# Sums of gated tiles: accumulating transfers into DRAM in place of VectorE additions

## The chip, the core and the metric

The kernel runs on one core of a Trainium2 chip. A core has TensorE (PE: matrix products into the accumulator memory PSUM), VectorE (DVE), ScalarE (ACT) and GpSimd (POOL) for work element by element, and SyncE (SP), which here only issues transfers. All of them run side by side, each works through its own queue in order, and they wait for one another by semaphores. A transfer (DMA) is carried out by 16 DMA engines once its issuing engine has reached it in its queue; a semaphore tells when it has landed. Working memory is SBUF with 128 partitions; DRAM is the large memory of the chip.

The metric is the time of one execution on the chip in microseconds (us). The three runs of the kernel before gave 1491.32, 1491.71 and 1492.59 us, median 1491.71.

## What is computed

A bidirectional encoder layer runs on two requests with shared weights: `x_prompt` (512 tokens) and `x_sample` (1024 tokens), both 1024 wide. The part that matters here is the feed-forward block at the end:

```python
x = x + jnp.concatenate([a_out, c], axis=-1) @ w_out[l]
h = _rmsnorm(x, norm_ffn_g[l])
u = _dwconv(h @ w_up[l], ffn_dw_w[l], ffn_dw_b[l])        # 3 taps along the tokens
x = x + (jax.nn.silu(u[..., :D_FF]) * u[..., D_FF:]) @ w_down[l]
return _rmsnorm(x, norm_final_g)
```

`D_FF` is 2816, that is 22 blocks of 128 columns, each with a gate half and a value half in `w_up`. Everything is float32; the products are made from two rounded parts of each operand, as three matrix products.

## The kernel before

**Stages.** The input projection, the attention and the convolution come first, then the prompt's up-projection, then the output projection of the sample, the sample's up-projection (a loop over the 22 blocks j, about 765 to 1135 us), and last the down-projection of both requests. This case is about the last two.

**Strassen's method.** Both of these stages multiply 2x2 blocks of matrices with seven products instead of eight (the form of Winograd). For the up-projection of a block j the seven products `first` to `seventh` are each twelve matmuls (four chunks of 128, three products of parts). Their order on PE is written out by hand, in the loop `for j in range(2, NJ)`: second(j), sixth(j), first(j+1), seventh(j), fifth(j+1), fourth(j), third(j). Their weight operands are sums of blocks of `w_up`: `sums_up` makes the sums on VectorE, and `split_up(j, i)` makes the two parts for product i: ScalarE casts the block (L1215), GpSimd subtracts the cast from the block (`sub` with `nc.gpsimd`, L1092). The raw weights are fetched three blocks ahead by `load_up` (L1179).

**Gate and value.** When the products of block j are there, `gate_part(j)` applies the convolution's taps to the gate half (`dwconv`, L1357 to L1359) and makes the tanh (L1366). One iteration later `value_part(j)` does the same for the value half and multiplies: L1376, `dwconv`, L1378. The result `t` is a tile of 128 columns (as partitions) by 1024 tokens; `L` and `R` are its two halves of 512 tokens.

**The sums in question.** For the down-projection, two neighbouring blocks (a pair p, even block e and odd block t) are the four quarters of a 2x2 block matrix: e[L], e[R], t[L], t[R]. Its seven products need seven operands per pair: three of the quarters themselves (e[L] as 1, t[L] as 2, t[R] as 4) and four sums of them (numbers 5, 7, 6, 3). In the kernel before, the even block's tile is kept in `even[p]`, and after the odd block VectorE makes the four sums; SP stores all seven in DRAM, each as a tensor of its own, `ga[i, p]`, 256 KB:

```python
add(x[:, R], e[:, R], t[:, R])          # 5
sub(x[:, L], e[:, L], e[:, R])          # 7
sub(e[:, R], x[:, R], e[:, L])          # 6
sub(y[:], t[:, L], e[:, R])             # 3
for i, b in ((5, x[:, R]), (7, x[:, L]), (6, e[:, R]), (3, y[:])):
    nc.sync.dma_start(ga[i, p][:], b)
```

`add` is L1089 and `sub` is L1092, helpers that many places call, so these lines stand for more than these sums. For the prompt's tokens `pair_sums` makes the same kind of sums on GpSimd (L1023 to L1029) into `gb`.

**Buffers.** `Slots` hands out SBUF buffers of fixed sizes by a list of the free ones: of those large enough it takes the smallest size, and in it the one that came back first (`next(...)` over `free`, and `give` appends). Tiles of 4 KB per partition take a `q` (4096 bytes) when one is free, else a `c` (4224 bytes). A buffer comes back when Python drops the last name of its tile; the new owner's first writer then waits for the old owner's last access. In an iteration the order of the 4 KB tiles is: two for `split_up(j+1, 1, 2)`, one for product 5, then in `value_part(j-1)` the value half's convolution tile, then one each for `split_up(j+1, 6)` and `split_up(j+1, 7)`, the two of `gate_part(j)`, and one each for products 4 and 3.

**Order of the work.** In this stage only PE's order is written by hand (`manual_schedule`); in the last block SP's as well. The orders of ACT, DVE, POOL and SP come from a planner that simulates the program, with dependences by tile, before it is compiled, and are fixed from then on.

**The down-projection.** `ahead` lists the loads of operands in the order of the products 1, 2, 5, 6, 7, 4, 3, for each of the eleven pairs; `load_next` issues them on SP (L1517 for operands of `ga`), long before `operands` uses them. `group` and `mm_down` run the products (L1579 to L1581), and `evacuate(i, w, z)` adds the product of PSUM to the running sums in SBUF.

Of the kernel before, what the change touches and what calls it, by code (L numbers as in the profile page):

```python
# [9 lines left out]
F32 = mybir.dt.float32  # L10
# [3 lines left out]
ALU = mybir.AluOpType  # L14

P = 128
D = 1024
KC = D // P
NT = 512
# [154 lines left out]
def tile_hybrid_encoder(ctx: ExitStack, tc: tile.TileContext, xs, xsT, rel_bias, norm_attn_g, w_in,  # L174
                        attn_sink, w_out, norm_ffn_g, w_up, w_down, norm_final_g, packed, onehot, outs):
    nc = tc.nc
# [5 lines left out]
    dr = ctx.enter_context(tc.tile_pool(name="dr", bufs=1, space=bass.MemoryType.DRAM))  # L182
# [8 lines left out]
    sb = Slots(lambda tag: homes[tag[0]], dict(q=(15, 4096), c=(4, 4224), h=(61, 2048), d=(2, 2176), s=(32, 64)), "q", KEEP)  # L191
# [793 lines left out]
    NPAIR = NJ // 2  # L985
# [4 lines left out]
    HL, HR = slice(0, HT), slice(HT, NT)  # L990

    def gate(j, a, b):
        th, t = bank("gate"), sb.tile([NT])
        nc.scalar.activation(th[:], a[:], AF.Tanh, scale=0.5)
        if j % 4 == VG:
            nc.vector.scalar_tensor_tensor(th[:], th[:], 1.0, a[:], op0=ALU.add, op1=ALU.mult)
            nc.vector.tensor_tensor(t[:], th[:], b[:], op=ALU.mult)
        else:
            nc.vector.scalar_tensor_tensor(t[:], th[:], 1.0, a[:], op0=ALU.add, op1=ALU.mult)
            nc.gpsimd.tensor_tensor(t[:], t[:], b[:], op=ALU.mult)  # L1000
        nc.sync.dma_start(gt[j // 2][:, j % 2, :], t[:])
        if j // 2 < SOON or j // 2 == NPAIR - 1:
            return
        if j % 2 == 0:
            evens[j // 2] = t
        else:
            for _ in pair_sums(j // 2, evens.pop(j // 2), t):
                pass
# [4 lines left out]
    def pair_sums(p, e=None, o=None):  # L1013
        if e is None:
            g = sb.tile([2, NT], among="c")
            nc.sync.dma_start(g[:], gt[p][:])
            yield 0.0
            yield 0.0
            e, o = g[:, 0, :], g[:, 1, :]
        r = sb.tile([4, HT], among="c")  # L1020
        gp = nc.gpsimd.tensor_tensor
        with tc.issue_after(ended["pool"]):
            gp(r[:, 0, :], e[:, HR], o[:, HR], op=ALU.add)  # L1023
        yield 0.0
        gp(r[:, 1, :], e[:, HL], e[:, HR], op=ALU.subtract)
        yield 0.0
        gp(r[:, 2, :], r[:, 0, :], e[:, HL], op=ALU.subtract)
        yield 0.0
        gp(r[:, 3, :], o[:, HL], r[:, 2, :], op=ALU.subtract)  # L1029
        nc.sync.dma_start(gb[p][:], r[:])  # L1030
        yield 0.0

# [52 lines left out]
    W2 = 2 * NT  # L1085
    L, R = slice(0, NT), slice(NT, W2)

    def add(out, a, b, eng=None):
        (eng or nc.vector).tensor_tensor(out, a, b, op=ALU.add)  # L1089

    def sub(out, a, b, eng=None):
        (eng or nc.vector).tensor_tensor(out, a, b, op=ALU.subtract)  # L1092
# [154 lines left out]

    side.extend((right_halves(), conv_norm(4 + NE)))
    side.extend(pair_sums(p) for p in (*range(SOON), NPAIR - 1))
    pace.update(rate=2.2)  # L1250
    for i in range(4, NB - 2):
# [41 lines left out]
    def wide():  # L1293
        return wide_banks.tile([W2])

    ga = {(i, p): dr.tile([P, NT], F32, name=f"ga{i}_{p}") for i in range(1, 8) for p in range(NPAIR)}
    st = {}

    def pair_banks(j):
# [54 lines left out]
    def dwconv(src, f):  # L1354
        w = lambda t: fw[:, t * 44 + f:t * 44 + f + 1]
        u = sb.tile([W2])
        nc.scalar.activation(u[:], src[:], AF.Identity, scale=w(1), bias=fb[:, f:f + 1])  # L1357
        nc.vector.scalar_tensor_tensor(u[:, 1:W2], src[:, 0:W2 - 1], w(0), u[:, 1:W2], op0=ALU.mult, op1=ALU.add)
        nc.vector.scalar_tensor_tensor(u[:, 0:W2 - 1], src[:, 1:W2], w(2), u[:, 0:W2 - 1], op0=ALU.mult, op1=ALU.add)  # L1359
        return u  # L1360
# [4 lines left out]
        t = s["t"] = sb.tile([W2])  # L1365
        nc.scalar.activation(t[:], ug[:], AF.Tanh, scale=0.5)  # L1366

    even = {}

    def value_part(j):  # L1370
        if j < 0:
            return
        p = j // 2
        s = st.pop(j)
        ug, t = s["ug"], s["t"]
        nc.vector.scalar_tensor_tensor(t[:], t[:], 1.0, ug[:], op0=ALU.add, op1=ALU.mult)  # L1376
        uv = dwconv(s.pop("wy"), NJ + j)
        nc.vector.tensor_tensor(t[:], t[:], uv[:], op=ALU.mult)  # L1378
        del ug, uv
        s.clear()  # L1380
        if j % 2 == 0:
            even[p] = t
            nc.sync.dma_start(ga[1, p][:], t[:, L])
            return
        e, x, y = even.pop(p), sb.tile([W2]), sb.tile([NT])
        for i, blk in ((2, L), (4, R)):
            nc.sync.dma_start(ga[i, p][:], t[:, blk])
        add(x[:, R], e[:, R], t[:, R])
        sub(x[:, L], e[:, L], e[:, R])
        sub(e[:, R], x[:, R], e[:, L])  # L1390
        sub(y[:], t[:, L], e[:, R])
        for i, b in ((5, x[:, R]), (7, x[:, L]), (6, e[:, R]), (3, y[:])):
            nc.sync.dma_start(ga[i, p][:], b)

# [79 lines left out]
    first(2)  # L1476
    split_up(2, 6)
    value_part(0)
    third(1)
    split_up(2, 7)  # L1480
# [10 lines left out]
    def load_next(n):  # L1491
        for _ in range(n):
            if ahead:
                key, p = ahead.popleft()
                roomy = sum(f[0][0] in "qc" for f in sb.free) > 5
                if (key, p) in second_half:
                    t = second_half.pop((key, p))
                elif key in BRIEF and p % 2 == 0 and p + 1 < NPAIR and roomy:
                    both = sb.tile([2, NT])
                    t, second_half[key, p + 1] = Part(both, 0), Part(both, 1)  # L1500
                    both = None
                else:
                    t = sb.tile([NT])
                pr[key, p] = t
                what, i, n2 = key
                if what == "a":
                    src = ga[i, p][:]
                elif what == "g":
                    n = min(2, NPAIR - 2 * p)
                    for q in range(n):  # L1510
                        j, h = {1: (0, HL), 2: (1, HL), 4: (1, HR)}.get(i, (0, None))
                        src = gb[2 * p + q][:, GB[i], :] if h is None else gt[2 * p + q][:, j, h]
                        nc.sync.dma_start(t[:, q * HT:(q + 1) * HT], src)
                    continue
                else:
                    src = w_down[0, (2 * p + i) * P:(2 * p + i + 1) * P, n2 * NT:(n2 + 1) * NT]
                nc.sync.dma_start(t[:], src)  # L1517
# [16 lines left out]
    def operands(i, p):  # L1534

        while (("a", i, 0), p) not in pr or (i in need and (need[i], p) not in pr) or \
                (p % 2 == 0 and (("g", i, 0), p // 2) not in pr):
            load_next(1)
# [54 lines left out]
    acc = {}  # L1593

    def evacuate(i, w, z):
        def at(name):
            return acc.setdefault(name, {})

        def fresh(name):
            t = at(name)[w] = sb.tile([W2])  # L1600
            return t

        if i == 1:
            nc.scalar.copy(fresh("u")[:], z[:])
        elif i == 2:
            add(fresh("o11")[:], z[:], acc["u"][w][:])
        elif i == 5:
            nc.scalar.copy(fresh("e")[:], z[:])
        else:
            u = acc["u"][w]  # L1610
            add(u[:], z[:], u[:])
            if i == 6:
                add(fresh("o12")[:], u[:], acc["e"][w][:], nc.gpsimd)
            elif i == 7:
                add(acc["e"][w][:], u[:], acc["e"][w][:], nc.gpsimd)

    def with_x(name, t, n):
        x = xd.pop((t, n))
# [45 lines left out]
    def group(i, p, w, lead=LEAD):  # L1664

        k = ORDER.index(i) * NPAIR + p
        if len(pr) < CAP and sum(f[0][0] == "h" for f in sb.free) > ROOM:
            load_next(1)
        make(k + lead)
        if w not in pd:  # L1670
            pd[w] = wide()
        for q in range(2):
            mm_down(pd[w][:, q * NT:(q + 1) * NT], i, p, 2 * w + q)
        left[i, p] = left.get((i, p), NW3) - 1
        if left[i, p] == 0:
            hl.pop((i, p))
            if p % 2 == 1 or p == NPAIR - 1:
                hp.pop((i, p // 2))
        if p == NPAIR - 1:
            evacuate(i, w, pd.pop(w))  # L1680
# [34 lines left out]
    for j in range(2, NJ):  # L1715
# [5 lines left out]
        if j >= NJ - 2:  # L1721
            load_next(4)
# [3 lines left out]
        sixth(j)  # L1726
        split_up(j + 1, 5)
        value_part(j - 1)
        last = j == NJ - 1
        if last:  # L1730
# [19 lines left out]
    fill((3, 0), (3, 1), (4, 0), (4, 1))  # L1750
    sb.free.extend(raws.free)
    value_part(NJ - 1)

    for i in ORDER[:-1]:
        product(i)
    with_x("u", 1, 0)
    u, e, o11, o12 = (acc.pop(n) for n in ("u", "e", "o11", "o12"))
# [26 lines left out]
    for tt in (2, 3):  # L1784
        z = wide()
# [60 lines left out]
```

## Time and profile before

| What | us |
|---|---|
| median of three runs | 1491.71 |
| the profiled execution, by its own time | 1492.24 |
| its span, first to last instruction | 1490.4 |
| TensorE busy | 1471.8 |
| VectorE busy | 1136.2 |
| ScalarE busy | 798.0 |
| GpSimd busy | 678.0 |

The granted clock of TensorE was 0.998 of full speed in the mean. DRAM was read with 165.29 MB and written with 60.05 MB. Every transfer of the program is issued by SP; GpSimd issues none.

How to read the rows: a busy time is that of the engine's own instructions; issuing a transfer and waiting don't count as busy. In rows by group the mean duration of one instruction is in ns. `q<-h,q 128x512` says which kind of buffer is written and which are read, and how large. `[0.72 <-DMA ga<-q]` at the end of a row is the time that the engine had stood idle before it and what ended that: here the landing of a transfer from a q tile to `ga`. A matmul's row lasts 0.39 us because matmuls are pipelined; the next one starts much sooner.

### The profile page before, as it was taken

Reading aid. Unit: us, or ns where it says so; the run is one execution under the profiler, and the core shown is the slowest. Engines: PE = TensorE matmul, PEld = TensorE weight load, DVE = VectorE, ACT = ScalarE, POOL = GpSimd, SP = SyncE. Lnnn points to the kernel's source line nnn. Section 1 sums busy time; section 2 is a strip of 40 time slices with the busy share of each in tenths; the row PEclk is TensorE's granted clock in tenths of the full one; section 3 lists DMA queues with packets and bytes.
Section 4 is the critical chain, followed back from the end, with each engine's and each line's share of the span. In section 5 each row is a group of like instructions: output and inputs, shape, how many; then the busy total and the mean of one; then the engine's idle time right before and its main releaser. Section 6 shows DMA issues by size and latency. Waiting matters only on the chain.

```text
span 1490.4 us, 19857 instructions
## 1 busy us (share of the span) xinstructions
PE 1471.8 (99%) x6808; PEld 1218.8 (82%) x6808; DVE 1136.2 (76%) x1616; ACT 798.0 (54%) x1417; POOL 678.0 (45%) x540
## 2 busy tenths in 40 slices
PE   9999999999999999999999999999999999999998
PEld 7788887887888888878888888888887888888886
DVE  5999996888689975666868777777776945569884
ACT  8555656345777776444465544555445633444254
POOL 6962335235665575763326555555544000003345
PEclk9999999999999999999999999999999999999999
DMA  9953246374433347883213333333332672357644
GB/s 316 284 171 92 86 121 184 99 231 128 133 110 121 120 126 224 272 304 131 82 57 106 106 106 106 106 104 99 103 105 80 227 265 85 113 171 233 216 163 170
DMA packets 221905, 225.60 MB, mean 151 GB/s; under 512 B 12347, under 2 KB 161859, under 8 KB 221676
## 3 DMA queue, kind: packets, MB, share of 16 engines
q1 hardware_dynamic: 221804, 224.34, 47.0%
q8 instruction: 53, 0.87, 0.3%
q14 instruction: 48, 0.39, 0.1%
HBM read 165.29 MB, written 60.05 MB: 151 GB/s over the span
## 4 chain that ended last, share of the span: by engine, by line
PE 86%; DMA 5%; DVE 3%; POOL 2%; ACT 1%; issue 1%; SPq 0%; POOLq 0%; ACTq 0%; DVEq 0%
PE w L1229 9%; PE w L1231 9%; PE w L1230 9%; PE w L1580 7%; PE w L1579 7%; PE w L1581 7%; PE u L347 4%; PE u L348 4%; PE u L350 4%; PE b L347 4%; PE b L350 4%; PE b L348 4%; DMA c<-gt 2%; PE u L840 2%; PE u L842 2%; PE u L841 2%
## 5 line engine op out<-in xcount | busy, mean ns | idle before, releaser
L231 POOL TENSOR_TENSOR q<-q,q 128x1024 fp32r<-128x1024 f32 x71 | 172.9, 2439 | 122.8 <-ACT q L230 51.4
L1092 POOL TENSOR_TENSOR q<-q,q 128x512 fp32r<-128x512 f32 x101 | 141.5, 1408 | 151.2 <-ACT q L1215 140.3
L1092 DVE TENSOR_TENSOR h<-h,h 128x512 fp32r<-128x512 f32 (+2 forms) x202 | 157.4, 814 | 65.6 <-ACT h L1096 27.8
L1581 PE MATMUL w<-h,h 128*128 128x512 f32 x462 | 179.7, 389 | 0.0
L1579 PE MATMUL w<-h,h 128*128 128x512 f32 x458 | 178.2, 389 | 0.0
L1580 PE MATMUL w<-h,h 128*128 128x512 f32 x458 | 178.2, 389 | 0.0
L1229 PE MATMUL w<-h,q 128*128 128x512 f32 x448 | 174.9, 390 | 1.3 <-ACT w L1312 1.1
L1231 PE MATMUL w<-h,q 128*128 128x512 f32 x448 | 174.3, 389 | 0.0
L1230 PE MATMUL w<-h,q 128*128 128x512 f32 x426 | 165.8, 389 | 0.0
L402 DVE SCALAR_TENSOR_TENSOR c<-c,cvw,c 128x512 f32<-128x512 f32 x209 | 157.0, 751 | 3.1
L347 PE MATMUL u<-h,q 128*128 128x512 f32 x368 | 146.9, 399 | 1.9 <-DVE h L969 1.9
L348 PE MATMUL u<-h,q 128*128 128x512 f32 x368 | 144.0, 391 | 0.0
L350 PE MATMUL u<-h,q 128*128 128x512 f32 x360 | 141.2, 392 | 0.0
L1089 POOL TENSOR_TENSOR q<-q,q 128x1024 f32<-128x1024 f32 x12 | 33.1, 2772 | 229.4 <-DVE q L1089 212.9
L1096 ACT CAST h<-h 128x512 fp32r<-128x512 f32 x120 | 72.1, 622 | 97.1 <-DVE h L1092 40.5
L347 PE MATMUL b<-h,q 128*128 128x512 f32 x264 | 104.9, 397 | 0.9 <-DVE q L437 0.9
L230 ACT CAST q<-q 128x1024 fp32r<-128x1024 f32 (+1 forms) x73 | 75.7, 1041 | 54.5 <-POOL q L231 20.6
L348 PE MATMUL b<-h,q 128*128 128x512 f32 x264 | 103.7, 393 | 0.0
L350 PE MATMUL b<-h,q 128*128 128x512 f32 x264 | 103.5, 393 | 0.0
L1581 PEld LDWEIGHTS w<-h,h 128*128 128x128 f32 x462 | 86.7, 188 | 18.0
L1579 PEld LDWEIGHTS w<-h,h 128*128 128x128 f32 x458 | 86.0, 188 | 18.0
L1580 PEld LDWEIGHTS w<-h,h 128*128 128x128 f32 x458 | 86.0, 188 | 17.7
(443 smaller groups left out, 3625.1 us busy)
## 6 DMA issues: line engine op xcount, KB each, us to landing
q<-in_w_up SPq DMA_DIRECT2D x88, 512.0 KB, 4.3
ga<-q SPq DMA_DIRECT2D x64, 256.0 KB, 2.0
h<-ga SPq DMA_DIRECT2D x57, 256.0 KB, 3.4
q<-in_w_in SPq DMA_DIRECT2D x28, 512.0 KB, 5.1
h<-in_w_down SPq DMA_DIRECT2D x52, 256.0 KB, 4.0
q<-in_x_sample SPq DMA_DIRECT2D x15, 512.0 KB, 6.2
h<-qsd SPq DMA_DIRECT2D x23, 256.0 KB, 3.3
x1d<-q SPq DMA_DIRECT2D x11, 512.0 KB, 5.2
```

The costliest lines, as they stand in the source:

```text
L231: ins = (nc.vector if dve else nc.gpsimd).tensor_tensor(lo[:], raw[:], hi[:].bitcast(F32), op=ALU.subtract)
L347: nc.tensor.matmul(out, whi[:, kc, :], hi[:], start=(kc == 0), stop=False)
L348: nc.tensor.matmul(out, whi[:, kc, :], lo[:], start=False, stop=False)
L350: nc.tensor.matmul(out, wlo[:, kc, :], hi[:], start=False, stop=(kc == KC - 1))
L402: nc.vector.scalar_tensor_tensor(acc[:], src(t), w(t), acc[:], op0=ALU.mult, op1=ALU.add)
L1092: (eng or nc.vector).tensor_tensor(out, a, b, op=ALU.subtract)
L1229: nc.tensor.matmul(out, whi[:, s], hi[:], start=(start and c == 0), stop=False, **go)
L1230: nc.tensor.matmul(out, whi[:, s], lo[:], start=False, stop=False, **go)
L1231: nc.tensor.matmul(out, wlo[:, s], hi[:], start=False, stop=(stop and c == 3), **go)
L1579: nc.tensor.matmul(out, sh[:, c], th[:], start=(p == 0), stop=False)
L1580: nc.tensor.matmul(out, sh[:, c], tl[:], start=False, stop=False)
L1581: nc.tensor.matmul(out, sl[:, c], th[:], start=False, stop=(p == NPAIR - 1))
```

## The change

For the sample's pairs the four sums are no longer made by VectorE. DRAM has a tensor `gs[p]` with four planes of 512 tokens for each pair. After the even block SP stores e[L] into the planes 0, 1 and 2 at once (one transfer that reads its source three times, 768 KB) and e[R] into plane 3. Then GpSimd issues a transfer that adds e[R] to the planes 0, 1 and 2 (`accum_op=ALU.add`). After the odd block GpSimd issues two more: t[R] is added to the planes 1, 2 and 3, and t[L] to plane 2. So the planes become e[L]+e[R], e[L]+e[R]+t[R], e[L]+e[R]+t[R]+t[L] and e[R]+t[R]. The operands 1, 2 and 4 are stored as before.

Compared with the sums before, e[L] and e[R] enter with the same sign in place of opposite ones: the second token half is turned, and so are the products that have it. `evacuate` takes that back by subtracting where it added, and `pair_sums` makes the prompt's sums with the same signs. The tile `even[p]` is no longer kept, and the tiles `x` and `y` are not needed.

```diff
@@ pair_sums
-        gp(r[:, 1, :], e[:, HL], e[:, HR], op=ALU.subtract)
+        gp(r[:, 1, :], e[:, HL], e[:, HR], op=ALU.add)
...
-        gp(r[:, 2, :], r[:, 0, :], e[:, HL], op=ALU.subtract)
+        gp(r[:, 2, :], r[:, 0, :], e[:, HL], op=ALU.add)
...
-        gp(r[:, 3, :], o[:, HL], r[:, 2, :], op=ALU.subtract)
+        gp(r[:, 3, :], o[:, HL], r[:, 2, :], op=ALU.add)
@@
-    ga = {(i, p): dr.tile([P, NT], F32, name=f"ga{i}_{p}") for i in range(1, 8) for p in range(NPAIR)}
+    ga = {(i, p): dr.tile([P, NT], F32, name=f"ga{i}_{p}") for i in (1, 2, 4) for p in range(NPAIR)}
+    gs = [dr.tile([P, 4, NT], F32, name=f"gs{p}") for p in range(NPAIR)]
+    GS = {7: 0, 6: 1, 3: 2, 5: 3}
@@
-    even = {}
+    def into(out, src):
+        nc.gpsimd.dma_start(out, src, accum_op=ALU.add)
+
+    def three(src):
+        return src.unsqueeze(1).to_broadcast([P, 3, NT])
@@ value_part
         if j % 2 == 0:
-            even[p] = t
             nc.sync.dma_start(ga[1, p][:], t[:, L])
+            nc.sync.dma_start(gs[p][:, 0:3, :], three(t[:, L]))
+            nc.sync.dma_start(gs[p][:, 3, :], t[:, R])
+            into(gs[p][:, 0:3, :], three(t[:, R]))
             return
-        e, x, y = even.pop(p), sb.tile([W2]), sb.tile([NT])
         for i, blk in ((2, L), (4, R)):
             nc.sync.dma_start(ga[i, p][:], t[:, blk])
-        add(x[:, R], e[:, R], t[:, R])
-        sub(x[:, L], e[:, L], e[:, R])
-        sub(e[:, R], x[:, R], e[:, L])
-        sub(y[:], t[:, L], e[:, R])
-        for i, b in ((5, x[:, R]), (7, x[:, L]), (6, e[:, R]), (3, y[:])):
-            nc.sync.dma_start(ga[i, p][:], b)
+        into(gs[p][:, 1:4, :], three(t[:, R]))
+        into(gs[p][:, 2, :], t[:, L])
@@ load_next
-                    src = ga[i, p][:]
+                    src = gs[p][:, GS[i], :] if i in GS else ga[i, p][:]
@@ evacuate
             u = acc["u"][w]
-            add(u[:], z[:], u[:])
             if i == 6:
-                add(fresh("o12")[:], u[:], acc["e"][w][:], nc.gpsimd)
+                sub(u[:], u[:], z[:])
+                sub(fresh("o12")[:], u[:], acc["e"][w][:], nc.gpsimd)
             elif i == 7:
-                add(acc["e"][w][:], u[:], acc["e"][w][:], nc.gpsimd)
+                add(u[:], z[:], u[:])
+                sub(acc["e"][w][:], acc["e"][w][:], u[:], nc.gpsimd)
+            else:
+                sub(u[:], z[:], u[:])
```

## The prediction

> **What bounds the kernel now.** I read the page first, then busy time by stretch, then what PE waited for, then the middle stage in order of time. The page:
>
> ```profile
> span 1490.4 us, 19857 instructions
> PE 1471.8 (99%) x6808; PEld 1218.8 (82%) x6808; DVE 1136.2 (76%) x1616; ACT 798.0 (54%) x1417; POOL 678.0 (45%) x540
> ```
>
> TensorE is busy for all but 18.6 us. The change touches the loop over the sample's 22 column blocks, and by signs and sources the stage behind it. The windows view (stretch, length, then busy us of each engine):
>
> ```profile
> 806.00:1120.00 314.00, 314.00 (x1386) 259.96 (x1386) 241.11 (x229) 158.83 (x231) 167.06 (x118) 1.00 0.32 103
> 1110.00:1135.00 25.00, 23.94 (x106) 19.49 (x105) 12.05 (x12) 12.43 (x19) 12.07 (x10) 1.00 0.11 33
> 1135.00:1300.00 165.00, 165.00 (x730) 136.59 (x729) 109.65 (x152) 75.89 (x122) 10.24 (x8) 1.00 0.52 170
> ```
>
> PE never pauses from 806 to 1120 us; a matmul starts every 314 / 1386 = 0.227 us, so one block (seven products of twelve matmuls) takes 84 x 0.2266 = 19.03 us and a pair 38.06. VectorE, from which work is taken, is busy 77% of it and bounds nothing. What PE waits for there in all (us, times, longest):
>
> ```profile
> PE w L1229 <- ACT w L1312: 1.1, 1, 1.1
> PE w L1229 <- ACT w L1330: 0.3, 1, 0.3
> ```
>
> **All that a faster VectorE can give back is 1.4 us**, 0.1% of the time. A measurement of this kernel tells about 0.2% (3 us) from no change, so a gain could hardly be seen. The question is whether the new transfers make PE wait.
>
> **What is removed.** Four VectorE sums per pair, in order of time around one odd block (start, us, instruction):
>
> ```profile
> 912.28 0.68 DVE L1092 TENSOR_TENSOR q<-q 128x512 f32<-128x512 f32 x1
> ...
> 915.16 1.21 DVE L1378 TENSOR_TENSOR q<-q,c 128x1024 f32<-128x1024 f32 x1
> ...
> 917.99 0.68 DVE L1089 TENSOR_TENSOR q<-q,q 128x512 f32<-128x512 f32 x1
> 918.70 0.69 DVE L1092 TENSOR_TENSOR q<-q,q 128x512 f32<-128x512 f32 x1
> 919.43 0.69 DVE L1092 TENSOR_TENSOR h<-q,q 128x512 f32<-128x512 f32 x1
> ```
>
> 0.68 + 0.68 + 0.69 + 0.69 = 2.74 us per pair, 30 us in eleven pairs, all beside a full PE: worth nothing but the 1.4 us above. L1378 at 915.16 makes the odd block's gated tile `t`, ready at 916.37. The even block's, with its store:
>
> ```profile
> 898.35 2.31 DVE L1378 TENSOR_TENSOR q<-q,c 128x1024 f32<-128x1024 f32 x1
> ```
>
> ```profile
> 900.68 0.34 SPq L1383 DMA_DIRECT2D ga<-q  x1
> ```
>
> ready at 900.66.
>
> **What costs nothing.** The turned signs in `evacuate` and `pair_sums` keep the number, shape and engine of each instruction. The loads of `gs` are as many as those of `ga` were, with the same 2 KB rows; they are issued a stage ahead of use, beside a PE at 165.00 of 165.00 us; if that cover went, each would cost a landing, 3.4 us (below). SP issues five stores per pair instead of seven. Traffic: before, 7 x 256 KB = 1.75 MB stored per pair; after, 1.75 MB by SP and 1.75 MB of accumulation, which is read and written in DRAM: 48 to 96 GB/s more over 38.06 us. At 103 GB/s the DMA engines are 0.32 busy, so that is 0.47 to 0.62: room is left, and the weights of `load_up` come three blocks ahead.
>
> **What is added: a chain behind `t`.** On an even block: the store of ga1, the threefold store into `gs` (768 KB), and only when that has landed GpSimd's accumulation of three right halves (A1). On an odd block: three right halves (A2), and when they have landed the left half into the third plane (A3), since it names bytes that A2 changes. No page row shows an accumulating transfer or one issued by POOL. The nearest issue rows (KB, us to landing):
>
> ```profile
> ga<-q SPq DMA_DIRECT2D x64, 256.0 KB, 2.0
> h<-ga SPq DMA_DIRECT2D x57, 256.0 KB, 3.4
> ```
>
> ```profile
> x1d<-c SPq DMA_DIRECT2D x1, 512.0 KB, 2.6
> ```
>
> A store costs 2.0 us and 0.6 for each further 256 KB: 3.2 for 768 KB. An accumulation is bounded below by that same store (nothing excludes that it costs no more), 3.2 and for A3 2.0; above by three loads and three stores of 256 KB one behind the other, 3 x (3.4 + 2.0) = 16.2. I take a read of 768 KB (3.4 + 2 x 0.6 = 4.6) and then its store (3.2): **7.8 us for A1 and A2, 3.4 + 2.0 = 5.4 for A3**. It is nearer to the lower end because one transfer's pieces overlap in the store rows. For POOL's issue I take one of its subtractions, 1.3 us, between SP's 0.34 and 2.4 (L231 on the page: 2439 ns):
>
> ```profile
> L231 POOL TENSOR_TENSOR q<-q,q 128x1024 fp32r<-128x1024 f32 x71 | 172.9, 2439 | 122.8 <-ACT q L230 51.4 <-issue 14.3 <-PE b L348 10.3
> ```
>
> **Who waits for the chain.** Not the loads, a stage later, but the next owner of `t`'s buffer. `Slots` hands out 4 KB buffers in the order in which they came back, q before c. That no q is free when `value_part` runs shows in its convolution tile, which is always a c:
>
> ```profile
> L1358 DVE SCALAR_TENSOR_TENSOR c<-w,fw,c 128x1023 f32<-128x1023 f32 x16 | 20.5, 1280 | 0.8
> ```
>
> So `ug` comes back first, then `t`; the next two tiles are those of `split_up(j+1, 6)` and `split_up(j+1, 7)`. Product 7's operands get `t`'s buffer, after even and odd blocks alike, and ScalarE's cast for them must wait until the last accumulation has read it. Such a wait is there already, for a plain store, and the cast and POOL's subtraction behind it read:
>
> ```profile
> 921.50 0.62 ACT L1215 CAST q<-h 128x512 fp32r<-128x512 f32 x1 [0.72 <-DMA ga<-q]
> ```
>
> ```profile
> 922.20 1.29 POOL L1092 TENSOR_TENSOR q<-h,q 128x512 fp32r<-128x512 f32 x1
> ```
>
> After an even block that cast ran at 896.70, before `t` was even finished, so here the wait is new:
>
> ```profile
> 896.70 0.62 ACT L1215 CAST q<-h 128x512 fp32r<-128x512 f32 x1
> ```
>
> Product 7 begins behind the product whose weights lie in a c tile; its third matmul is the first to read what POOL made:
>
> ```profile
> 914.51 0.39 PE L1231 MATMUL w<-h,c 128*128 128x512 f32 x1
> 914.74 0.39 PE L1229 MATMUL w<-h,q 128*128 128x512 f32 x1
> 914.96 0.39 PE L1230 MATMUL w<-h,q 128*128 128x512 f32 x1
> 915.19 0.39 PE L1231 MATMUL w<-h,q 128*128 128x512 f32 x1
> ```
>
> **The sum, even block:** 900.66, two issues 0.68, ga1 ahead in the queue 0.6, store 3.2: 905.1. A1: 1.3 + 7.8: 914.2. Cast 0.62, subtraction 1.29, hand-over 0.08: 916.2, against 915.19: **1.0 us late**. **Odd block:** 916.37 + 1.3 + 7.8 + 1.3 + 5.4 = 932.2, + 2.0 = 934.2, against 915.19 + 19.03 = 934.2: just in time. Ten pairs have a product 7 behind them (blocks 0 to 19): 10 x 1.0 = 10 us. PE is the clock of this loop, so what it loses isn't made up. Less at most 1.3 of the waits above: 1492.2 (the profiled execution, 1490.4 of span and 1.8 around it) + 10 - 1.3 = 1500.9; the median is 0.5 below that execution: **about 1500 us**.
>
> POOL is 53% busy in the loop (167.06 of 314), and three issues add 3.9 us per pair. Behind a waiting A3 on POOL's queue stand its subtractions; who waits for them is the third rival.
>
> **The rivals.**
>
> *No change, 0.35: 1490 to 1494.* An accumulation lands like a plain store. Even block: 905.1 + 1.3 + 3.2 + 2.0 = 911.6, 3.6 us ahead of 915.19; odd, 916.37 + 1.3 + 3.2 + 1.3 + 2.0 + 2.0 = 926.2, 8 ahead. PE never waits and the time stays at 1491. For it speaks how narrow my sum is: 7.8 needs only to be 6.8. Against it, that bytes are read and written in one transfer, and that ScalarE's order is fixed beforehand.
>
> The Trainium skill, "DMA: Bandwidth & Descriptors", section "Anatomy of one DMA — SWDGE (gpsimd) path", fits a transfer from GpSimd as 2.0 us and its bytes at 436 GB/s. An estimate by that page is 3.8 us for 768 KB, and the sum would be that of this rival; no run here shows it, and the page does not say that it holds for accumulation.
>
> *Faster, 0.04: 1487.* The mechanism would be VectorE's 2.74 us per pair. It needs PE waits on VectorE, and the rows give 1.4 us; only a better order in the stretch 1110 to 1135 and at the end could add to that.
>
> *Much slower, 0.21: 1520 to 1670.* Two forms. The accumulation takes longer: at 11 us the even block is 4.2 late and the odd one 3.2, 74 us in ten pairs, 1565; at the upper end of 16.2 it is 9.4 + 8.4, 178 us, about 1670. Or a queue stands still: POOL waits for A2 to land with A3 at its head, or ScalarE with product 7's cast, while what PE needs soon stands behind. On POOL these are:
>
> ```profile
> 920.86 1.30 POOL L1092 TENSOR_TENSOR q<-q,q 128x512 fp32r<-128x512 f32 x1 [3.34 <-ACT q L1215]
> ...
> 923.45 2.74 POOL L1092 TENSOR_TENSOR q<-q,q 128x512 fp32r<-128x512 f32 x2
> 926.52 1.30 POOL L1092 TENSOR_TENSOR q<-q,q 128x512 fp32r<-128x512 f32 x1 [0.33 <-ACT q L1215]
> ```
>
> A2 lands at 916.37 + 9.1 = 925.5, A3 is issued at 926.8, and then 1.3 + 1.29 + 2.74 + 1.30 us of subtractions end at 933.4. The last of them feeds product 1, which PE starts a product (2.72) before product 7: its third matmul is at 931.5. 1.9 us late per pair, 19 more: 1520. On ScalarE the copies L1312 and L1330 stand so; both rows of PE's waits name them, so they have little to spare.
>
> **How the numbers follow.** Forecast (late by a microsecond or two per pair, 1495 to 1520): 0.40. No change 0.35, much slower 0.21, faster 0.04. Slower by over 0.2% is 0.40 + 0.21 = 0.61, within 0.2% 0.35, faster 0.04. The range begins at 1489, which takes in most of the unchanged case (the 1.4 us and a little of measurement), and ends at 1565, the accumulation of 11 us; beyond it and below it I leave out some 0.15. Slower cases hold most of the chance; the forecast's own range is 1495 to 1520.
>
> **What would show it.** Right: PE has some ten waits of about a microsecond in 806 to 1130, released by POOL's or ScalarE's part of product 7 (`q<-h`); those casts are released by a DMA that reads q into `gs`; the accumulations land about 8 us after their issue. VectorE's four groups above are gone and its busy time is 30 us less. Wrong: PE stays full over the loop (no change); or its waits name L1312, L1330 or other subtractions of POOL (a queue that stands still); or they stand in the stage behind 1135, where I see none.

## The result and the profile after

The changed kernel takes **1579.94 us** in the median of five runs (1575.83 to 1581.39); beside it the kernel before took 1492.59 (1491.32 to 1493.94). The ratio is 1.0581, with a 95% interval of 1.0565 to 1.0598: slower by 87 us, where 1500 was forecast and 1565 was the upper end of the range.

The page of the changed kernel, its first lines:

```profile
span 1578.2 us, 19826 instructions
...
PE 1502.2 (95%) x6808; PEld 1230.3 (78%) x6808; DVE 1094.3 (69%) x1572; ACT 792.6 (50%) x1417; POOL 704.4 (45%) x573
```

The span grew by 87.8 us. TensorE's time without work grew from 18.6 to 76.0 us, by 57.4. Its busy time grew by 30.4 us though it runs the same 6808 matmuls: the other part of the loss is matmuls that took longer. The windows view of the loop shows both (stretch, length, busy us of PE, PEld, DVE, ACT, POOL, granted clock, DMA share, GB/s):

```profile
806.00:860.00 54.00, 39.68 (x146) 30.98 (x145) 26.29 (x23) 17.96 (x26) 20.91 (x17) 0.84 0.50 122
860.00:1000.00 140.00, 126.88 (x534) 99.77 (x533) 74.29 (x73) 57.70 (x88) 67.83 (x52) 0.99 0.53 125
1000.00:1110.00 110.00, 97.54 (x390) 76.61 (x389) 56.91 (x56) 43.84 (x65) 51.80 (x41) 0.93 0.54 124
...
806.00:1120.00 314.00, 274.09 (x1106) 215.45 (x1105) 161.88 (x156) 122.59 (x184) 145.80 (x112) 0.94 0.53 124
```

In the same 314 us TensorE starts 1106 matmuls, where it had started 1386. TensorE stands idle for 40 of them, no other engine is near its limit, and the DMA engines are half idle: this loop waits. The pace of a pair is seen in SyncE's store of two even blocks in succession, 45.3 us apart (38.06 before):

```profile
884.48 0.34 SPq L1389 DMA_DIRECT2D ga<-q  x1
...
929.80 0.34 SPq L1389 DMA_DIRECT2D ga<-q  x1
```

What ended the waits from 806 to 1220 us (engine, line, releaser: us in all, times, longest):

```profile
POOL gs L1371 <- DMA gs<-q: 60.6, 14, 7.2
...
ACT q L1215 <- issue: 43.5, 7, 7.6
ACT q L1215 <- DMA gs<-q: 42.4, 9, 6.3
...
PE w L1229 <- DVE q L1361: 17.1, 3, 7.7
PE w L1231 <- POOL q L1092: 17.1, 13, 1.5
...
PE w L1229 <- ACT q L1215: 10.3, 9, 2.3
```

Two queues stand at the accumulating transfers: GpSimd with its next transfer (60.6 us) and ScalarE with a cast. ScalarE's wait is in two rows. The profile names the landing for nine waits (42.4 us), eight of them at product 7's cast. For seven more it names no releaser ("issue", 43.5 us), but all seven are at that same cast and of 4.9 to 7.6 us, so the cast waited 81.1 us in 15 waits. In the kernel before, the same cast's waits for stores were these:

```profile
ACT q L1215 <- DMA ga<-q: 6.6, 8, 1.9
```

PE never waits for the transfers themselves, but for what comes behind those two queues. L1361 is the last step of a convolution on VectorE, whose first step is ScalarE's L1359; its three waits lie at the two ends of the loop. Which queue costs the time can't be read from these sums; the experiments tell. ScalarE in order of time, around two casts of product 7:

```profile
896.01 0.62 ACT L1215 CAST q<-h 128x512 fp32r<-128x512 f32 x1 [5.25 <-DMA gs<-q]
...
919.07 0.62 ACT L1215 CAST q<-h 128x512 fp32r<-128x512 f32 x1 [6.33 <-DMA gs<-q]
919.60 0.61 ACT L1215 CAST q<-q 128x512 fp32r<-128x512 f32 x1
920.12 1.20 ACT L1359 ACTIVATE c<-w,vecs,fw 128x1024 f32<-128x1024 f32 x1
```

`q<-h` is product 7's operand. ScalarE stands 5.25 us at the one and 6.33 at the other. Behind it stand the cast `q<-q` for product 1, which PE takes up a product **before** product 7, and a convolution (L1359). Now TensorE at the same place:

```profile
918.77 0.39 PE L1231 MATMUL w<-h,q 128*128 128x512 f32 x1
920.26 0.50 PE L1229 MATMUL w<-h,q 128*128 128x512 f32 x1 [1.11 <-ACT q L1215]
920.60 0.40 PE L1230 MATMUL w<-h,q 128*128 128x512 f32 x1
922.33 0.50 PE L1231 MATMUL w<-h,q 128*128 128x512 f32 x1 [1.33 <-POOL q L1092]
```

This is product 1: its first matmul starts 0.05 us after the cast of 919.60 has ended, its third waits for GpSimd's part of the same operand. Product 7, for whose operand ScalarE had waited, starts only at 925.56; GpSimd's part of that operand has been there since 921.04:

```profile
919.77 1.27 POOL L1092 TENSOR_TENSOR q<-h,q 128x512 fp32r<-128x512 f32 x1 [1.39 <-ACT q L1215]
```

```profile
925.56 0.50 PE L1229 MATMUL w<-h,q 128*128 128x512 f32 x1 [0.67 <-ACT h L1323]
```

### The profile page after: what moved, and what is told of

Same layout as the page of the kernel before. It is cut to its first block, busy times and chain, and to the rows that moved or that the text cites. A ratio compares the mean times of both kernels' runs of the same rounds, so it can differ in the third digit from the quotient of the medians.

```text
span 1578.2 us, 19826 instructions
## 1 busy us (share of the span) xinstructions
PE 1502.2 (95%) x6808; PEld 1230.3 (78%) x6808; DVE 1094.3 (69%) x1572; ACT 792.6 (50%) x1417; POOL 704.4 (45%) x573
## 4 chain that ended last, share of the span: by engine, by line
PE 64%; DMA 10%; POOL 8%; issue 8%; DVE 7%; ACT 3%; SPq 0%; POOLq 0%; DVEq 0%; ACTq 0%
PE w L1584 7%; PE w L1585 7%; PE w L1583 7%; DMA gs<-q 6%; PE u L347 4%; PE u L348 4%; PE u L350 4%; POOL q L1092 3%; PE b L347 3%; PE b L348 3%; PE b L350 3%; PE w L1229 3%; PE w L1230 3%; PE w L1231 3%; DMA q<-in_w_up 2%
## 5 line engine op out<-in xcount | busy, mean ns | idle before, releaser
L1092 POOL TENSOR_TENSOR q<-q,q 128x512 fp32r<-128x512 f32 (+1 forms) x115 | 171.9, 1550 | 271.5 <-DMA h<-gb 147.8
L1229 PE MATMUL w<-h,q 128*128 128x512 f32 x480 | 196.8, 410 | 37.0 <-DVE q L1361 19.2
L1231 PE MATMUL w<-h,q 128*128 128x512 f32 x480 | 195.1, 406 | 17.1 <-POOL q L1092 17.1
L1092 DVE TENSOR_TENSOR h<-h,h 128x512 fp32r<-128x512 f32 (+2 forms) x202 | 155.0, 801 | 70.5 <-ACT h L1096 28.1
L1230 PE MATMUL w<-h,q 128*128 128x512 f32 x458 | 184.5, 403 | 0.0
L1229 PEld LDWEIGHTS w<-h,q 128*128 128x128 f32 x480 | 94.2, 196 | 66.7 <-ACT q L1215 20.6
L1231 PEld LDWEIGHTS w<-h,q 128*128 128x128 f32 x480 | 93.9, 196 | 43.3 <-POOL q L1092 23.2
L1230 PEld LDWEIGHTS w<-h,q 128*128 128x128 f32 x458 | 89.9, 196 | 18.4
L1585 PEld LDWEIGHTS w<-h,h 128*128 128x128 f32 x462 | 86.7, 188 | 17.8
```

What stands on the lines that cost most here:

```text
L1229: nc.tensor.matmul(out, whi[:, s], hi[:], start=(start and c == 0), stop=False, **go)
L1230: nc.tensor.matmul(out, whi[:, s], lo[:], start=False, stop=False, **go)
L1231: nc.tensor.matmul(out, wlo[:, s], hi[:], start=False, stop=(stop and c == 3), **go)
L1585: nc.tensor.matmul(out, sl[:, c], th[:], start=False, stop=(p == NPAIR - 1))
```

## The experiments

Four theories were put to the test.

- **Theory 1**, the buffer as the prediction had it: product 7's operand is late because its buffer is read until the last accumulation has landed. A buffer that is kept longer would cure it.
- **Theory 1b**: the planner puts the cast where a plain transfer would have landed; the accumulation lands later; so ScalarE's queue stands, and what is behind the cast makes PE wait.
- **Theory 2**: GpSimd's queue stands with the next transfer, and its subtractions are late.
- **Theory 3**: the traffic of the accumulations, or the lower clock, costs by itself.

Line numbers in the experiments are a few higher where lines were added. Each ratio, and each difference to the kernel before, is to runs of that kernel beside the same experiment (medians 1490.95 to 1492.59 us).

| Kernel | median us | ratio to the kernel before, interval |
|---|---|---|
| changed kernel | 1579.94 | 1.0581 (1.0565 to 1.0598) |
| e1, tile kept a block longer | 1572.41 | 1.0554 (1.0537 to 1.0571) |
| e6, kept two blocks longer | 1570.81 | 1.0535 (1.0521 to 1.0550) |
| e2, without the last transfer | 1560.02 | 1.0475 (1.0455 to 1.0494) |
| e13, cast moved behind the tanh | 1535.54 | 1.0289 (1.0274 to 1.0304) |
| e9, as e6, cast bound | 1514.58 | 1.0156 (1.0129 to 1.0183) |
| e5, plain transfers | 1502.36 | 1.0084 (1.0070 to 1.0098) |
| e7, as e1, cast bound | 1502.29 | 1.0074 (1.0060 to 1.0088) |
| e14, as e7, plain transfers | 1488.78 | 0.9988 (0.9979 to 0.9998) |
| e3, before without its sums | 1492.74 | 1.0019 (1.0009 to 1.0030) |
| e4, before with the signs | 1491.74 | 1.0005 (0.9996 to 1.0014) |
| e12, before, cast bound | 1490.22 | 0.9993 (0.9984 to 1.0002) |

### Is it the accumulating? Plain transfers in the same order

```diff
     def into(out, src):
-        nc.gpsimd.dma_start(out, src, accum_op=ALU.add)
+        nc.gpsimd.dma_start(out, src)
```

> The changed kernel with GpSimd's 33 transfers as plain stores instead of accumulations, so that the sums are left out; ScalarE's and GpSimd's instructions stand in the same order as in after. If the accumulation's own time is the loss (landing 7.7 us for 768 KB where a plain store from SP takes 3.7), theories 1 and 2 both see each wait shorten by about 4 us, from 5.3 to 1 or 2, and the time falls to 1500 to 1520. If any transfer from GpSimd takes as long, or the chain of three is too long by itself, it stays at 1560 to 1580. Theory 3 by traffic: half of the added DRAM traffic goes, about 1535.

1502.36 us, 11 over the kernel before: 76 of the 87 us are gone. This kernel leaves the sums out. The fixed orders of ScalarE and of GpSimd are the same, instruction for instruction, in this kernel and in the changed one, so the planner tells an accumulation from a plain transfer in neither queue. The chip does. The row of the issues on the page (KB, median us to landing), first of the changed kernel:

```profile
gs<-q POOLq DMA_DIRECT2D x21, 768.0 KB, 7.7
```

and of this run:

```profile
gs<-q POOLq DMA_DIRECT2D x21, 768.0 KB, 4.3
```

The same 768 KB from the same engine land in 4.3 us plain and in 7.7 accumulating, counted from the start of the issue: 3.4 us more. For A3's 256 KB it is 2.7 and 4.2. And ScalarE at the same two places of its queue:

```profile
894.62 0.62 ACT L1215 CAST q<-h 128x512 fp32r<-128x512 f32 x1 [0.28 <-DMA gs<-q]
...
914.91 0.62 ACT L1215 CAST q<-h 128x512 fp32r<-128x512 f32 x1 [1.54 <-DMA gs<-q]
```

With the plain landing the cast stands where it hardly waits, 0.28 and 1.54 us. GpSimd, though, still waits long at `gs`, 70.5 us from 806 to 1220:

```profile
POOL gs L1371 <- DMA gs<-q: 70.5, 17, 24.0
...
ACT q L1215 <- DMA gs<-q: 6.6, 7, 1.5
```

(Waits without a releaser add 3.2 us here.) 76 us have gone with ScalarE's wait, while GpSimd's is no shorter in all: against theory 2.

### Theory 1: keep the buffer

```diff
+    lasting = deque()
...
         s.clear()
+        lasting.append(t)
+        if len(lasting) > 1:
+            lasting.popleft()
```

> The changed kernel, but each block's tile t is kept by name for one block longer, so that its buffer comes back when the accumulations that read it have long landed; the same transfers, computation whole. Theory 1 (buffer): ScalarE stood still at product 7's cast because it writes into t's buffer, 16 waits of about 5.3 us in the profile of after, and PE waited for what stands behind it on ScalarE; then these waits go and the time falls to 1491 to 1505. Theory 2 (GpSimd's queue): PE waited because GpSimd stands still until earlier transfers have landed (60.6 us in 14 waits at L1371); these waits stay, and the time stays at 1555 to 1580. Theory 3 (the transfers' traffic, and the lower granted clock): stays at about 1580.

1572.41 us: theory 1 in its simple form falls. With a block more of time before the buffer is used again, the wait at the cast did not go but grew, from 81.1 us to 124.6 (119.0 below, and 5.6 without a releaser; waits from 806 to 1220):

```profile
ACT q L1215 <- DMA gs<-q: 119.0, 16, 11.1
...
PE w L1229 <- ACT c L1359: 28.0, 6, 5.1
```

In order of time, the cast now stands 4 to 5 us in one block and about 10 in the next, and both convolutions are behind it:

```profile
910.03 0.62 ACT L1215 CAST q<-h 128x512 fp32r<-128x512 f32 x1 [10.54 <-DMA gs<-q]
910.55 1.20 ACT L1359 ACTIVATE q<-w,vecs,fw 128x1024 f32<-128x1024 f32 x1
...
913.71 1.20 ACT L1359 ACTIVATE c<-w,vecs,fw 128x1024 f32<-128x1024 f32 x1 [0.93 <-DVE w L1089]
```

A reading that fits: the older buffer let the planner put the cast earlier, up to where it thinks that buffer's transfers have landed, so that what was gained in the buffer was spent in the order. From this came theory 1b, which the next run tests.

### Theory 1b: the same, with the cast's place fixed

```diff
-            nc.scalar.copy(hi[:], src)
+            with (tc.issue_after(ended["p5"]) if i == 7 and j > 2 else nullcontext()):
+                nc.scalar.copy(hi[:], src)
...
-            nc.scalar.copy(s["p5"][:], s["wy"][:, L])
+            ended["p5"] = nc.scalar.copy(s["p5"][:], s["wy"][:, L]).ins
```

with the lines of `lasting` as above. ScalarE may take product 7's cast only behind its copy of the fifth product.

> As e1_hold_t, and ScalarE's cast for product 7 may stand in the queue only behind the copy of the same iteration's fifth product. In e1 ScalarE waited 119 us in 16 waits at that cast for transfers into gs, although its buffer had one block more: the planner had moved the cast forward, to where it takes the accumulation to have landed. Theory 1b (the planner counts an accumulation like a plain transfer, so that any cast whose buffer hangs on one stands at the head of ScalarE's queue some microseconds too early): the cast now comes 15 us or more after the accumulation's issue, its waits go, and the time falls to 1491 to 1510. Theory 2 (GpSimd's queue): GpSimd's waits at its transfers stay (61.7 us in 15 in e1), and with them 1555 to 1575. Theory 3 (traffic): 1570.

1502.29 us, 70 less than without the binding, with all accumulations in place. From 860 to 1100 us PE is full again, at the full clock:

```profile
860.00:1100.00 240.00, 240.00 (x1056) 197.27 (x1055) 157.05 (x152) 118.76 (x176) 135.64 (x106) 1.00 0.64 153
```

and the waits from 806 to 1220 us are these:

```profile
POOL gs L1374 <- DMA gs<-q: 67.6, 17, 6.7
...
PE w L1232 <- POOL q L1092: 3.7, 1, 3.7
PE w L1230 <- ACT w L1315: 2.1, 2, 1.4
```

GpSimd waits at its transfers as long as ever, 67.6 us, and PE has full work beside it: this wait is harmless there (against theory 2). The DMA engines carry 153 GB/s at a share of 0.64, more than in the changed kernel, beside the full clock (against theory 3).

The binding by itself, in the kernel before:

```diff
+            with (tc.issue_after(ended["p5"]) if i == 7 and j > 2 else nullcontext()):
+                nc.scalar.copy(hi[:], src)
```

> The kernel before with the same binding of product 7's cast behind the copy of the fifth product, nothing else. If the binding costs nothing by itself: 1490-1493. If it is what the 11 us of the bound runs come from: about 1500.

1490.22 us, ratio 0.9993 (0.9984 to 1.0002): it costs nothing and brings nothing that can be told.

### The order alone, on the same buffers

```diff
-        split_up(j + 1, 7)
+        split_up(j + 1, 7, later=(kept := []))
         fourth(j)
         gate_part(j)
         split_up(j + 1, 4)
+        for hi, lo, held in kept:
+            with tc.issue_after(ended["tanh"]):
+                nc.scalar.copy(hi[:], held[:])
+            sub(lo[:], held[:], hi[:].bitcast(F32), nc.gpsimd)
...
-        nc.scalar.activation(t[:], ug[:], AF.Tanh, scale=0.5)
+        ended["tanh"] = nc.scalar.activation(t[:], ug[:], AF.Tanh, scale=0.5).ins
```

`later` makes `split_up` take the tile at the old place and leave out the cast and the subtraction.

> The changed kernel with one place moved: product 7's cast on ScalarE (and GpSimd's subtraction behind it) is issued behind the tanh of the gate half instead of in front of its convolution tap, on the same buffers; transfers, sums and buffers as in the changed kernel. Theory 1b (what costs is that ScalarE stands at this cast while product 1's cast and the convolution tap stand behind it): PE's waits on ScalarE and on what follows from it go, and the time falls to 1490-1510; what is left of the wait at the cast is at most 3-4 us a block and harmless, since only the casts for products 4 and 1 of a later block stand behind it. If the accumulations cost by themselves (product 7's own operand late, GpSimd's queue, traffic or the clock): 1550-1580, with product 7's own third matmul waiting for GpSimd.

1535.54 us, 44 over the kernel before: the place alone gives back half of the 87 us. It is 25 above the upper figure for theory 1b and 15 below the other theories' lower one. The trace says why. In the middle of the loop the cast (L1758 here) waits little (one of them below, 22.9 us in 13 waits over the loop), and PE is 137.84 of 140 us busy:

```profile
894.26 0.62 ACT L1758 CAST q<-h 128x512 fp32r<-128x512 f32 x1 [0.26 <-DMA gs<-q]
```

```profile
860.00:1000.00 140.00, 137.84 (x603) 112.53 (x602) 90.79 (x84) 67.16 (x97) 81.78 (x61) 1.00 0.62 143
```

So there product 7's own operand was in time on the old buffers, and what the changed kernel lost in the middle was the cast's place in the queue. The rest is lost mostly at both ends of the loop, where PE has four waits for a convolution, 20.6 us in all. Two of them come from ScalarE: another tile, that of the convolution, gets `t`'s buffer, and ScalarE stands at its L1362 (L1359 in the changed kernel). Of ScalarE's two such waits, 9.9 us in all, this is the first, and PE behind it:

```profile
851.62 1.20 ACT L1362 ACTIVATE q<-w,vecs,fw 128x1024 f32<-128x1024 f32 x1 [5.05 <-DMA gs<-q]
```

```profile
856.67 0.77 PE L1232 MATMUL w<-h,q 128*128 128x512 f32 x1 [6.64 <-DVE q L1364]
```

The first pair has a third way, by GpSimd's queue. Its second and third transfer hold up a subtraction; a buffer for weights comes free late; SyncE's load (L1179) waits up to 9.9 us behind a subtraction, where in the kernel before it had been 5.8; and VectorE stands at its sum of weights:

```profile
811.23 1.29 POOL L1374 DMA_DIRECT2D gs<-c  x1 [5.25 <-DMA gs<-q]
...
819.10 0.91 POOL L1374 DMA_DIRECT2D gs<-c  x1 [5.28 <-DMA gs<-c]
```

```profile
820.30 4.04 DVE L1092 TENSOR_TENSOR h<-q 128x512 f32<-128x512 f32 x1 [13.15 <-DMA q<-in_w_up]
```

PE then waits 6.19 us at 828. Theory 2 holds there, for one pair. In the changed kernel PE has four waits for the same convolution at the same ends, of 4.5, 7.7, 5.0 and 6.6 us.

### Less on GpSimd's queue, and a later issue

Without the odd block's last transfer:

```diff
         into(gs[p][:, 1:4, :], three(t[:, R]))
-        into(gs[p][:, 2, :], t[:, L])
```

> The changed kernel without the last accumulation of a pair (t[L] into plane 2 is left out of operand 3's sum). Theory 1: the odd block's buffer is free some 3 us earlier (issue 0.9, landing 2.2), the even block's as before: 3 us in each of ten pairs, 1545 to 1555. Theory 2: GpSimd's longer wait of a pair (5.2 us behind A2) goes altogether and only the one of 2.3 us for the first store is left: 1500 to 1525. Theory 3: 1575.

1560.02 us, in none of the ranges named and nearest to theory 1's. GpSimd's wait at `gs` falls from 60.6 to 17.5 us and what is lost by only 18, to 69; ScalarE's wait is still there, 81.6 us in the row that names the landing:

```profile
ACT q L1215 <- DMA gs<-q: 81.6, 15, 8.2
...
POOL gs L1371 <- DMA gs<-q: 17.5, 7, 3.8
```

The tile kept for two blocks and each pair's first and last transfer issued a block later, so that nothing should land behind another:

```diff
+        while waiting:
+            into(*waiting.popleft())
         if j % 2 == 0:
...
-            into(gs[p][:, 0:3, :], three(t[:, R]))
+            waiting.append((gs[p][:, 0:3, :], three(t[:, R])))
```

> The changed kernel with t kept for two blocks longer, and the accumulation of an even block and the last one of an odd block issued a block later, when what they wait for has long landed; the product 7 cast is not bound to a place. GpSimd has nothing to wait for at its transfers but its own t. Theory 1b: the planner still moves the cast forward to where it takes the last accumulation to have landed, so ScalarE's waits stay, 1550 to 1575. Theory 2: GpSimd's waits go, 1491 to 1510.

1570.81 us, as e1; ScalarE's waits at the cast are 91.0 us (57.9, and 33.1 without a releaser). GpSimd's waits at `gs`, which this run was to remove, are still 57.5 us, so it does not tell theory 2 from 1b. The same with the cast bound by e7's lines:

```diff
+            with (tc.issue_after(ended["p5"]) if i == 7 and j > 2 else nullcontext()):
+                nc.scalar.copy(hi[:], src)
```

> e6_hold_later and the bound cast of e7_hold_pin together, computation whole: no wait of ScalarE or of GpSimd on an accumulation should be left in the loop. Theory 1b and theory 2: 1490 to 1495, what the forecast gave for accumulations that nobody waits for, at most 1.4 us below the kernel before. Theory 3 (the traffic or the issues by themselves cost): above 1510.

1514.58 us: a miss, 12 slower than e7 and in the range named for theory 3. Traffic by itself isn't shown by it, since e7 makes the same transfers in 1502. Binding took 56 us off e6, as 1b has it, but issuing later brought nothing: GpSimd waits 80.3 us at `gs`, more than in e7, and PE has eight waits of up to 1.4 us for a copy of ScalarE's. Why these come was not followed further.

### What e7 still loses

```diff
-        nc.gpsimd.dma_start(out, src, accum_op=ALU.add)
+        nc.gpsimd.dma_start(out, src)
```

in e7's kernel, which so leaves the sums out.

> The run with the tile held a block longer and the cast bound, but with GpSimd's 33 transfers plain instead of accumulating (the sums are left out). It tells whether the 11 us that were left there belong to the accumulation. If they do (the landing of 7.7 us makes GpSimd wait at the second transfer, one late subtraction and the slower clock behind it): 1491-1494. If they come from binding the cast or from holding the buffer: 1500-1503 again.

1488.78 us, 2 below the lower range named: e7's last 11 us (over the kernel before; 13.5 over this run) belong to the accumulation too. From 765 to 1220 us the profile names no wait of PE here. In e7's profile it waited 3.7 us for a subtraction at 818 us, behind the first pair's third transfer, and had the slower clock after it:

```profile
806.00:860.00 54.00, 49.52 (x206) 39.85 (x205) 32.62 (x31) 24.88 (x36) 30.25 (x24) 0.94 0.62 132
```

### What the change takes away, and the signs

The kernel before without the four sums on VectorE, its quarters stored in their place:

```diff
-        add(x[:, R], e[:, R], t[:, R])
-        sub(x[:, L], e[:, L], e[:, R])
-        sub(e[:, R], x[:, R], e[:, L])
-        sub(y[:], t[:, L], e[:, R])
```

> The kernel before without VectorE's four sums per pair; quarters are stored in the place of the sums, so seven stores per pair as before, and no accumulation. This is the whole of what the change could win on VectorE. By the forecast's bound (1.4 us of PE waits in the loop): 1490 to 1492.5 beside 1492.6 of before, ratio 0.999 to 1.000, with PE as full as before and VectorE 30 us less busy. If VectorE bounds something that the rows don't show: below 1488.

1492.74 us, ratio 1.0019 (1.0009 to 1.0030), a little above the range named. VectorE is 200.92 us busy from 806 to 1120, where it was 241.11, and the time is not less:

```profile
806.00:1120.00 314.00, 312.82 (x1380) 258.71 (x1379) 200.92 (x195) 155.15 (x227) 151.67 (x113) 1.00 0.32 103
```

The signs alone, in the kernel before (`pair_sums`, `evacuate` and the four sums turned as in the change):

```diff
-        sub(x[:, L], e[:, L], e[:, R])
-        sub(e[:, R], x[:, R], e[:, L])
-        sub(y[:], t[:, L], e[:, R])
+        add(x[:, L], e[:, L], e[:, R])
+        add(e[:, R], x[:, R], e[:, L])
+        add(y[:], t[:, L], e[:, R])
```

> The kernel before with the signs of the change alone: sums by VectorE with e[L] and e[R] of one sign, evacuate and pair_sums as in after, no accumulation, computation whole. All theories, and the forecast, which put this part at nothing: 1490 to 1493, ratio 0.998 to 1.002.

1491.74 us, ratio 1.0005: nothing.

## Why the prediction was wrong

The forecast was slower by about 8 us; measured were 87. The buffer, the waiting cast and most sizes were right, the wait that costs the time was not. By its steps:

- **What is removed is worth nothing: right.** e3 takes it away alone and gains nothing. (VectorE's busy time fell by 41.9 us in the changed kernel, not by 30; it bounds nothing either way.)
- **Signs cost nothing: right.** e4.
- **Landing of 7.8 us for A1 and A2, 1.3 us to issue: right as single figures, but added up.** Measured were 7.7, and 1187 ns for an issue (mean of the 26 from a q tile, 765 to 1220 us). But the profile counts the landing from the start of the issue, so the 1.3 us are part of the 7.7, where the sum has 9.1 for both. For A3 it has 6.7 and 4.2 were measured. Whether an accumulation is a read and then a store, as was assumed, no run shows.
- **Traffic has room: right.** The share was 0.53 in the changed kernel, and 0.64 beside a full PE in e7.
- **Who waits for the chain: right in the buffer.** Product 7's cast waits for `gs<-q`, after even and odd blocks. The chain came out shorter than estimated: on the even block from SyncE's store at 884.48 to the cast at 896.01 it took 11.5 us, where 900.68 to 914.2 (13.5 us) was worked out; nearly all of the difference lies between A1's issue at 888.77 and its landing, 7.2 us where the sum has 9.1.
- **The step that failed is "The sum".** It set the end of the chain only against product 7's own third matmul: 1.0 us late on even blocks, in time on odd ones, 10 us in all. In the rows at 919 to 926 us that operand was there 4.5 us before its product began. What the sum left out is what stands **behind** the waiting cast on ScalarE: product 1's cast and a convolution. The text named it ("ScalarE with product 7's cast, while what PE needs soon stands behind"), among the forms of "much slower" at 0.21 in all, priced the form on GpSimd at 1520, and left this one without a price. Moving the cast alone gave back 43 of the 87 us (e13); keeping the buffer and binding the cast gave back 76 (e7). The part that e13 did not give back lies mostly at the ends of the loop, where `t`'s buffer goes to a convolution's tile and, for one pair, GpSimd's queue holds up the weights. The text had neither of the two.
- **That "slower" came true is luck as far as the sum goes.** With the measured 7.7 and 4.2 its own working ends at 905.1 + 7.7 + 2.0 = 914.8 against 915.19, and at 916.37 + 7.7 + 4.2 + 2.0 = 930.3 against 934.2: in time on both blocks, no change. The sign named for "right" seems to be there, 13 waits of PE of 1.3 us in the mean for GpSimd, but the rows above show one of them at product 1's operand, not at product 7's.
- **An estimate of the price, made afterwards.** A planner that takes an accumulation for a plain transfer puts the cast where the "no change" rival has it land: 911.6 - 2.0 = 909.6 and 926.2 - 2.0 = 924.2. The forecast's landing lets it run at 914.2 and 932.2. The queue would stand for the differences, 4.6 + 8.0 = 12.6 us per pair; the rows above show 5.25 + 6.33 = 11.6. That it comes so near is in part luck: with the measured landings the differences are 7.7 - 4.3 = 3.4 and 3.4 + 4.2 - 2.7 = 4.9, 8.3 us, and against e5's waits of 0.28 and 1.54 the measured ones are 9.8 longer. A pair takes 45.3 - 38.06 = 7.2 us longer, the slower clock included; the rest would be slack in front of the operands. No run tests this working by itself.
- **"No change" was weighed with the wrong argument.** "ScalarE's order is fixed beforehand" stood as a doubt in half a sentence; it was most of the case. e5 and the changed kernel have the same order, and 76 us lie between what they lose.
- **The rival on GpSimd, 1520,** is seen in the first pair only. Elsewhere GpSimd stands for 60 to 70 us without harm (e7, e5).
- **The clock was not in the sum.** TensorE's busy time grew by 30.4 us, a third of the loss. An estimate from the mean clocks, 0.017 x 1578.2 - 0.002 x 1490.4, puts 24 of them down to the clock. The upper end of 1565 left it out; it fell 15 us short.

What is inferred and not shown: how the planner prices a transfer. That it treats both kinds alike follows from the equal orders. The binding without the kept buffer was not run; e13 is the nearest to it. What exactly slows e9 stays open.

No kernel here that makes the sums is faster than the kernel before by more than its interval. Where PE is at 314.00 of 314.00 us and VectorE's sums are hidden, the change had nothing to win: e14, where these transfers do no adding, is 0.12% below the kernel before (0.02 to 0.21), and no run shows more to be had.

## What to carry to other kernels

Where a change makes one instruction wait longer, price first what is queued behind it on its engine, then the instruction's own consumer: here the consumer had 4.5 us to spare and the queue behind had none. Where a planner fixes the order beforehand, an operation that lands later than it reckons with can turn up as a stall of a queue in which it placed the next user too early; here a buffer kept longer didn't cure this (e1), a moved place cured half (e13), and both together most of it (e7). And work taken off an engine that bounds nothing is worth only the waits on it, so any new wait at all is too much.

## What was not expected of the hardware

**An accumulating transfer lands much later than a plain one of its size:** 7.7 us against 4.3 for 768 KB from GpSimd, and 4.2 against 2.7 for 256 KB. GpSimd's issue is longer too, 1.29 us against 0.79 in these rows, the first from the changed kernel and the second from e5:

```profile
888.77 1.29 POOL L1371 DMA_DIRECT2D gs<-q  x1 [2.30 <-DMA gs<-q]
```

```profile
887.36 0.79 POOL L1371 DMA_DIRECT2D gs<-q  x1 [1.98 <-DVE q L1385]
```

The plain landing of 4.3 us is near the 3.8 us that the prediction estimated by the Trainium skill's page "DMA: Bandwidth & Descriptors", section "Anatomy of one DMA — SWDGE (gpsimd) path"; the accumulating one, 7.7 us, is twice that.

**The clock falls after pauses of a few microseconds, and its price comes on top of the pauses:** about 24 us here, beside 57 us of pauses. In e13, around the pause that ended at 828 us (columns as in the windows above):

```profile
814.00:821.00 7.00, 7.00 (x31) 5.80 (x32) 0.70 (x1) 1.25 (x2) 1.90 (x3) 1.00 0.95 180
821.50:828.00 6.50, 0.37 (x2) 0.00 (x0) 6.42 (x5) 0.00 (x0) 2.28 (x2) 0.80 0.71 189
828.00:831.50 3.50, 3.44 (x8) 2.79 (x9) 1.23 (x2) 3.15 (x4) 1.81 (x1) 0.50 0.02 5
```

Before the pause 31 matmuls start in 7 us; behind it PE is busy all the time and starts 8 in 3.5 us, where 15 or 16 would be usual, at half the clock. In the changed kernel shorter pauses did it too: in the stretch from 1000 to 1020 us PE has two waits, of 2.34 and 1.33 us with two matmuls between them, and the granted clock was 0.83:

```profile
1000.00:1020.00 20.00, 16.33 (x59) 12.65 (x58) 10.13 (x10) 7.09 (x10) 9.02 (x8) 0.83 0.52 104
```

The Trainium skill, "TensorE: Matmul & The Clock Gate", section "What's actually happening", has the clock halved after an idle window of about 3.4 us and back after a busy one; the pause that ended at 828 us fits that, but from 1000 to 1020 us two shorter pauses close together were enough. In the kernel before, whose PE hardly ever paused, the mean clock was 0.998; after the change it was 0.983, and the mean matmul `w<-h,q` of L1231 rose from 389 to 406 ns.
